# A hybrid decoder layer on one core: the up product of the MLP by Strassen's scheme, the down sums added in DRAM

## The chip, the core and the metric

The kernel runs on one core of a Trainium2 chip. The metric is the device time of one execution in microseconds; the time before is the median of three runs. A second, profiled execution gives the page and the trace that the text reads. Engines are called as the profile calls them: PE (matrix product), PEld (its weight load), DVE (vector), ACT (scalar, activations), POOL (GpSimd), SP (the queue that issues most DMAs).

## The reference

One layer over 2064 tokens (16 meta tokens and 2048 inputs) of width 1024. A first half (input projection, gated convolution, a state-space group, output projection) leaves a residual stream h. The change touches the second half only:

```
hn = rms_norm(h, norm_ffn_g)
up = causal_dwconv(hn @ w_up, ffn_conv_w, ffn_conv_b)   # 1024 -> 2 x 2816, depthwise, width 3
a, val = up[..., :2816], up[..., 2816:]                 # gate and value
h = h + (silu(a) * val) @ w_down                        # 2816 -> 1024
y = rms_norm(h, norm_final_g)[:, 16:]
```

All arrays are float32. Each product of two float32 matrices is computed as three: both factors are split into a high and a low part of type fp32r, and hi·hi, hi·lo and lo·hi are summed in PSUM.

## The kernel before

Activations lie with features on the 128 partitions and tokens along the free axis. Tokens are cut into three blocks (`BLOCKS`: 676 rows, then 688 and 688, with a halo of two carried from block to block in `halo_z`), each block into two chunks `c` of 338 or 344 columns. A matmul has a 128x128 weight tile and one chunk of columns.

Weights arrive by `Stream`: a DMA on SP into a raw tile (`wr`), a copy to fp32r on ACT (`wh`, the high part), a subtraction on DVE (`wl`, the low part). Five tiles are held ahead, two of them already split.

The MLP of a block runs over 22 tiles `f` of 128 hidden features, and for each over `i` = 0 (gate) and 1 (value). `up(f, i)` takes one weight tile, runs 8 feature groups x 2 chunks x 3 products = 48 matmuls into one PSUM tile (`product`, lines 135, 136 and 139), copies it to `z` on ACT (line 1135), and makes the convolution: one ACT operation (line 1136) and two DVE operations (`axpy`, line 111). The gate then gets Silu on ACT; the value is multiplied with it on DVE, copied to fp32r on ACT (`ah`) and subtracted on DVE (`al`).

After a chunk of hidden tiles (`FF_CHUNKS` = 6, 5, 5, 6 of the 22) the down product of that chunk runs: `down(ci, (m,))` for eight output tiles m, each 6 matmuls per hidden tile, and DVE adds each PSUM result to `acc`, a resident SBUF copy of the residual (line 105, acc<-dn,acc). The table `plan` puts this down product behind the up product of the first hidden tile of the next chunk; only the last chunk of a block has no such tile ahead of it. PSUM is held in three tiles of two banks (`ps_mm`) and two aux banks.

`prep_mlp(b + 1)` loads the next block's h, takes its norm and splits it into `h_f` and `l_f`; `finish` takes the final norm of a block from `acc` and stores y. Both are generators that `prep.step` advances a piece at a time between the products. For block 0 `prep_mlp` runs beside the last output projection of the first half, `out_block(2, ...)`. The order of the instructions on each engine is set by a scheduler from this program.

Of the kernel before, what the change touches and what calls it, by code (L numbers as in the profile page):

```python
# [50 lines left out]
FF_CHUNKS = (6, 5, 5, 6)  # L51
# [6 lines left out]
def layer_kernel(ctx, tc, xq, pk, w_in, w_glu, w_out, w_up, w_down, ssm_s, ssm_m, y):  # L58
# [8 lines left out]
    xp_ = ctx.enter_context(tc.tile_pool(name="xp_", bufs=1))  # L67
# [50 lines left out]
    def split_weights(raw, nk, name):  # L118
        hi = wp.tile([P, KD, P], F32R, tag="wh", bufs=4, name=f"wh_{name}")
        lo = wp.tile([P, KD, P], F32R, tag="wl", bufs=4, name=f"wl_{name}")  # L120
        S.activation(hi[:, :nk, :], raw[:, :nk, :], AF.Copy)  # L121
        tt(lo[:, :nk, :], raw[:, :nk, :], f32(hi[:, :nk, :]), ALU.subtract)
        return hi, lo
# [86 lines left out]

    def scaled(src, c0, rs, n, name, view=None):
# [24 lines left out]

    def norm_split(res, loads, n, cols, name):

        xs = load_halves(loads, n, name)
        yield  # L240
        yield
        rs = yield from inv_rms(xs, n, name)
        out = []
        for i, t in enumerate(xs):
            yield
            hi, lo = hl_tile(n, f"h_{name}_{i}"), hl_tile(n, f"l_{name}_{i}")
            split(t, cols[i], rs, hi, lo, n, f"{name}_{i}")
            out.append((hi, lo))
        res.append(out)
# [32 lines left out]
    prep, ssm = Side(), Side()  # L282

# [51 lines left out]
    def down_items(b, ci, tag=""):  # L335
        f0, nk = chunk_of[ci]
        return [(w_down[m, :, f0 : f0 + nk, :], nk, f"dn{b}_{ci}_{m}{tag}") for m in range(KD)]

    for b in range(3):
        for p in plan:  # L340
            if p[0] == "up":
                items.append((w_up[p[2] * FT + p[1]], KD, f"up{b}_{p[1]}_{p[2]}"))
            else:
                items += down_items(b, p[1])
        items += down_items(b, len(ends) - 1)
    items += down_items(2, len(ends) - 1, "b")
# [656 lines left out]
    def prep_mlp(b, res):  # L1003
        first, ni, _ = BLOCKS[b]
        n = ni // 2
        for c in range(2):
            s0 = first + c * n
            yield from norm_split(
                res, (h_d[:, 0:4, s0 : s0 + n], h_d[:, 4:8, s0 : s0 + n]), n, (C_FFN, C_FFN + 4), f"f{b}{c}"
            )  # L1010

    hg, hf = ([[] for _ in range(3)] for _ in range(2))
# [68 lines left out]
    prep.add(prep_mlp(0, hf[0]))  # L1081
    out_block(2, both(2), KD)
    prep.drain()
    es_2.close()


    fp = ctx.enter_context(tc.tile_pool(name="fp", bufs=1))
    ZB, MAX_OUT = 690, 688
    halo = fp.tile([P, 2 * FT, 2], F32, name="halo_z")

    def finish(b, acc, c):
        tb, ni, no = BLOCKS[b]
        n = no // 2
        halves = [acc[:, i * 4 : i * 4 + 4, c * n : (c + 1) * n] for i in range(2)]
        s = sum_squares(halves, n, f"y{b}{c}")
        yield
        rs = yield from inv_rms_of(s, D, n, f"y{b}{c}")
        yield
        s0 = tb + ni - no - META + c * n
        for k in range(KD):  # L1100
            a = acc[:, k, c * n : (c + 1) * n]
            V.scalar_tensor_tensor(out=a, in0=a, scalar=col(C_FIN + k), in1=rs, op0=ALU.mult, op1=ALU.mult)
            if k % 2 == 1:
                dma(out=y[:, k - 1 : k + 1, s0 : s0 + n], in_=acc[:, k - 1 : k + 1, c * n : (c + 1) * n])
# [12 lines left out]

    for b in range(3):
        tb, ni, no = BLOCKS[b]
        n, nn = ni // 2, no // 2  # L1120
        while len(hf[b]) < 2:
            prep.step()
        rhs = rhs_of(hf[b])
        act, br = {}, {}
        acc = None

        def up(f, i):
            t = i * FT + f
            ps = mm_tile(f"up_{b}_{f}_{i}")
# [24 lines left out]
        def down(ci, ms, cs=(0, 1)):  # L1154
# [4 lines left out]
            def rhs_down(k, i):  # L1159
                return tuple(x[:, cs[i] * nn : (cs[i] + 1) * nn] for x in act[f0 + k])  # L1160
# [8 lines left out]
        for p in plan:  # L1169
# [114 lines left out]
```

## Time and profile before

| what | us |
|---|---|
| median of 3 runs (2275.03 to 2276.7) | 2275.16 |
| the profiled execution, its own time | 2274.12 |
| its span, first to last instruction | 2272.3 |
| first `up` matmul starts at | 758.4 |
| busy in the span: PE / DVE / ACT / POOL | 2203.6 / 1329.5 / 883.2 / 34.3 |
| mean granted TensorE clock | 0.987 |

The page's groups give a line of the kernel, the engine, the operation with its tiles, the number of instructions, their busy time and the mean of one in ns, and then the idle time of the engine ahead of them with what ended it. Matmuls overlap in the records, so the mean duration of one (320 ns) is not its cost; the cost is the time of a stretch over the matmuls in it.

### The profile page before, as it was taken

The numbers are of one execution on the slowest core, as the hardware profiler recorded it, in microseconds if no ns is written. First come the engines' busy times: TensorE is split into PE (matmuls) and PEld (weight loads), VectorE is DVE, ScalarE is ACT, GpSimd is POOL, SyncE is SP. The second block draws the span as 40 slices with busy tenths as digits, with TensorE's granted clock in tenths as the row PEclk, the third lists the DMA queues.
The fourth block names the chain that finished last, engine by engine and source line by source line (L and its number), as shares of the span: only waits on it lengthen the run. The fifth ranks groups of instructions, "written<-read, shape, count | busy, mean of one in ns | idle before, by whom it ended". The sixth has DMA issues, their size and how long they took to land.

```text
span 2272.3 us, 32764 instructions
## 1 busy us (share of the span) xinstructions
PE 2203.6 (97%) x13798; PEld 2178.6 (96%) x13798; DVE 1329.5 (59%) x1911; ACT 883.2 (39%) x1175; POOL 34.3 (2%) x38
## 2 busy tenths in 40 slices
PE   4999999989899999999999999999999999999998
PEld 3998999988899999999999999999999999999997
DVE  7877499857956554444456663535356553444446
ACT  3244333227523442424244542424244442424243
POOL 0000000000000000000000000000000000000000
PEclk8999999999899999999999999999999999999999
DMA  5475444352475422231214232121223242121313
GB/s 189 121 234 146 135 146 153 116 174 65 136 241 180 167 63 77 61 88 52 88 58 132 90 133 82 54 87 54 86 61 92 90 131 84 50 90 49 91 53 118
DMA packets 134676, 245.38 MB, mean 108 GB/s; under 512 B 29120, under 2 KB 83072, under 8 KB 134400
## 3 DMA queue, kind: packets, MB, share of 16 engines
q1 hardware_dynamic: 133376, 239.05, 34.6%
q10 hardware_dynamic: 1152, 4.23, 0.5%
q8 instruction: 108, 1.77, 0.3%
q14 instruction: 40, 0.33, 0.0%
HBM read 206.94 MB, written 36.31 MB: 107 GB/s over the span
## 4 chain that ended last, share of the span: by engine, by line
PE 87%; DVE 7%; DMA 2%; ACT 2%; issue 1%; POOL 0%; SPq 0%; POOLq 0%; DVEq 0%; ACTq 0%
PE up L136 15%; PE up L135 15%; PE up L139 15%; PE dn L136 7%; PE dn L135 7%; PE dn L139 7%; PE po L135 2%; PE po L136 2%; PE po L139 2%; PE cc L136 1%; PE cc L135 1%; PE pu L136 1%; PE cc L139 1%; PE pu L139 1%; PE pu L135 1%
## 5 line engine op out<-in xcount | busy, mean ns | idle before, releaser
L135 PE MATMUL up<-h_f,wh_up 128*128 128x344 f32 (+1 forms) x2112 | 671.1, 320 | 0.0
L136 PE MATMUL up<-l_f,wh_up 128*128 128x344 f32 (+1 forms) x2112 | 669.3, 320 | 0.0
L139 PE MATMUL up<-h_f,wl_up 128*128 128x344 f32 (+1 forms) x2112 | 505.1, 318 | 0.0
L135 PEld LDWEIGHTS up<-h_f,wh_up 128*128 128x128 f32 x2112 | 397.6, 188 | 0.4
L136 PEld LDWEIGHTS up<-l_f,wh_up 128*128 128x128 f32 x2112 | 397.5, 188 | 0.4
L139 PEld LDWEIGHTS up<-h_f,wl_up 128*128 128x128 f32 x2112 | 365.7, 189 | 0.0
L135 PE MATMUL dn<-ah,wh_dn 128*128 128x344 f32 (+1 forms) x1008 | 319.8, 320 | 0.1
L136 PE MATMUL dn<-al,wh_dn 128*128 128x344 f32 (+1 forms) x1008 | 318.7, 319 | 0.0
L105 DVE TENSOR_TENSOR wl_up<-wr_up,wh_up 128x1024 fp32r<-128x1024 f32 x132 | 161.5, 1223 | 242.2 <-ACT wh_up L121 242.2
L121 ACT ACTIVATE wh_up<-wr_up 128x1024 fp32r<-128x1024 f32 x132 | 140.0, 1060 | 371.5 <-PE up L136 189.2
L111 DVE SCALAR_TENSOR_TENSOR t<-z,pv,t 128x688 f32<-128x688 f32 (+1 forms) x264 | 245.3, 929 | 66.2 <-ACT t L1136 61.9
L139 PE MATMUL dn<-ah,wl_dn 128*128 128x344 f32 (+1 forms) x1008 | 242.8, 318 | 0.0
L105 DVE TENSOR_TENSOR acc<-dn,acc 128x688 f32<-128x688 f32 (+2 forms) x104 | 84.5, 813 | 224.2 <-PE dn L139 224.2
L135 PEld LDWEIGHTS dn<-ah,wh_dn 128*128 128x128 f32 x1008 | 189.3, 188 | 0.8 <-ACT ah L1150 0.4
L136 PEld LDWEIGHTS dn<-al,wh_dn 128*128 128x128 f32 x1008 | 189.6, 188 | 0.4
L139 PEld LDWEIGHTS dn<-ah,wl_dn 128*128 128x128 f32 x1008 | 174.4, 188 | 0.0
L121 ACT ACTIVATE wh_dn<-wr_dn 128x768 fp32r<-128x768 f32 (+1 forms) x96 | 75.5, 791 | 228.4 <-PE dn L136 139.9
L105 DVE TENSOR_TENSOR wl_dn<-wr_dn,wh_dn 128x768 fp32r<-128x768 f32 (+1 forms) x96 | 85.1, 888 | 120.0 <-ACT wh_dn L121 112.0
L1136 ACT ACTIVATE t<-z,pv 128x688 f32<-128x688 f32 (+1 forms) x132 | 126.5, 959 | 1.5
L1150 ACT ACTIVATE ah<-t 128x688 fp32r<-128x688 f32 (+1 forms) x66 | 51.0, 773 | 159.1 <-DVE t L105 159.0
L1144 ACT ACTIVATE t<-t 128x688 f32<-128x688 f32 (+1 forms) x66 | 51.2, 776 | 125.7 <-DVE t L111 125.7
L121 ACT ACTIVATE wh_cw<-wr_cw 128x1024 fp32r<-128x1024 f32 x36 | 38.1, 1059 | 153.6 <-PE cc L136 44.0
(354 smaller groups left out, 3438.2 us busy)
## 6 DMA issues: line engine op xcount, KB each, us to landing
wr_up<-in_w_up SPq DMA_DIRECT2D x132, 512.0 KB, 3.5
wr_cw<-in_w_in SPq DMA_DIRECT2D x36, 512.0 KB, 4.6
wr_dn<-in_w_down SPq DMA_DIRECT2D x48, 384.0 KB, 3.2
wr_dn<-in_w_down SPq DMA_DIRECT2D x48, 320.0 KB, 2.9
x_c<-in_xq SPq DMA_DIRECT2D x16, 688.0 KB, 4.7
xr<-in_xq SPq DMA_DIRECT2D x24, 344.0 KB, 4.0
h_d<-xr SPq DMA_DIRECT2D x24, 344.0 KB, 3.2
wr_o<-in_w_out SPq DMA_DIRECT2D x16, 512.0 KB, 4.9
```

Of the source, the lines that this page charges most:

```text
L105: V.tensor_tensor(out, a, b, op=op)
L111: V.scalar_tensor_tensor(out=out, in0=a, scalar=s, in1=b, op0=ALU.mult, op1=ALU.add)
L121: S.activation(hi[:, :nk, :], raw[:, :nk, :], AF.Copy)
L135: T.matmul(ps[c], hi[:, k, :], xh, start=k == 0, stop=False)
L136: T.matmul(ps[c], hi[:, k, :], xl, start=False, stop=False)
L139: T.matmul(ps[c], lo[:, k, :], xh, start=False, stop=k == nk - 1)
L1136: S.activation(a, z[:, nz - no :], AF.Identity, scale=col(C_FW + 2 * 44 + t), bias=col(C_FB + t))
L1144: S.activation(a, a, AF.Silu)
L1150: S.activation(hi, a, AF.Copy)
```

## The change

The up product of one hidden tile is now a 2x2 block product: rows are gate and value, the inner dimension is the lower and the upper four of the eight feature groups, columns are the two token chunks. Strassen's scheme in Winograd's form makes it with seven half products instead of eight. Each half product (`form`) is 4 feature groups x 3 products = 12 matmuls of one chunk, so a hidden tile has 84 matmuls instead of 96. For this

- the seven right factors b11, t1, t2, b21, t3, t4, b22 are made once per block from the four quarters of the normed block (`prep_mlp`), and each is split into two fp32r parts held in 14 tiles `xf`;
- the seven left factors are made for each hidden tile: four DMAs bring the weights into three raw tiles, four DVE additions of 128x512 make the sums (`Pair.sums`), and three tiles of 1024 columns and one of 512 (`w4`) are split, where two of 1024 were;
- the results are put together outside PE: three ACT copies and four DVE additions from PSUM for each hidden tile (`up`), instead of two ACT copies. One partial sum in PSUM (X) is read by ACT while its accumulation goes on later; Y is read likewise by DVE.

The sign of the value row is taken into negated convolution weights (`pneg`). `Feed` replaces `Stream` in the MLP: at most three raw and four split tiles, refilled as a split tile is released. PSUM is two tiles of two banks (`xy`), two of one bank (`pz`) and the two aux banks. The work behind the up product of a hidden tile (`activate`) is a generator in three parts that runs within the next hidden tile's forms.

The hidden tiles are cut into chunks of 4, 4, 4, 3, 3 and 4, and a chunk's down product follows its own last up product (`settle` first); its first two output tiles share the loop (`first_pair`), so that the chunk's last hidden tile comes last in both. The result of a down product is no longer added by DVE to an SBUF tile: ACT copies it to `ev` (two buffers), and a DMA issued by POOL adds it to h in DRAM (`accum_op`). Only the last chunk of the last block still adds in SBUF. `finish` and the norm of the next block (`prep_rs`) read h back from DRAM. `prep_mlp` of block 0 cannot run beside `out_block(2, ...)` any more: its tiles lie in pools opened after that.

```diff
-FF_CHUNKS = (6, 5, 5, 6)
+FF_CHUNKS = (4, 4, 4, 3, 3, 4)
...
+    prep.add(prep_rs(0))
     out_block(2, both(2), KD)
     prep.drain()
     es_2.close()
+    es_x.close()
+    es_ps.close()
...
+    xf = ctx.enter_context(tc.tile_pool(name="xf", bufs=1, side="right"))
     fp = ctx.enter_context(tc.tile_pool(name="fp", bufs=1))
+    ps_xy = ctx.enter_context(tc.tile_pool(name="ps_xy", bufs=2, space=bass.MemoryType.PSUM))
+    ps_z = ctx.enter_context(tc.tile_pool(name="ps_z", bufs=2, space=bass.MemoryType.PSUM))
...
+        def sums(self):
+            self.t.append(fp.tile([P, 4, P], F32, tag="w4", bufs=1, name=f"w4_{self.name}"))
+            t = self.t
+            tt(t[0][:, 4:8, :], t[2][:, 4:8, :], t[2][:, 0:4, :], ALU.add)
+            tt(t[1][:, 0:4, :], t[0][:, 4:8, :], t[0][:, 0:4, :], ALU.add)
+            tt(t[2][:, 4:8, :], t[2][:, 4:8, :], t[0][:, 0:4, :], ALU.add)
+            tt(t[3], t[1][:, 0:4, :], t[1][:, 4:8, :], ALU.add)
...
+        def done(k, a):
+            hi, lo = (xf.tile([P, 4, QM], F32R, tag="xf", bufs=14, name=f"{w}_{k}_{b}")[:, :, :n] for w in "hl")
+            parts(a, hi, lo)
+            res[k] = (hi, lo)
...
+        done("b11", a)
+        tt(a, a, b12, ALU.subtract)
+        done("t1", a)
...
+        def form(ps, w, h, k, start=True, stop=True):
+            hi, lo = (a[:, h * 4 : h * 4 + 4, :] for a in w)
+            xh, xl = x[k]
+            for j in range(4):
+                kw = dict(skip_group_check=not (start and stop))
+                T.matmul(ps, hi[:, j, :], xh[:, j, :], start=start and j == 0, stop=False, **kw)
+                T.matmul(ps, hi[:, j, :], xl[:, j, :], start=False, stop=False, **kw)
+                T.matmul(ps, lo[:, j, :], xh[:, j, :], start=False, stop=j == 3, **kw)
...
+        def up(f):
...
+            w0 = feed.take()
+            form(X, w0, 0, "b11", stop=False)
+            S.activation(g2[:, 0, :], X, AF.Copy)
+            work()
+            form(Y, w0, 1, "t1", stop=False)
+            feed.done()
+            w1 = feed.take()
+            form(X, w1, 0, "t2", start=False, stop=False)
+            S.activation(g2[:, 1, :], X, AF.Copy)
+            work()
+            form(z1, w1, 1, "b21")
+            tt(g2[:, 0, :], z1, g2[:, 0, :], ALU.add)
+            feed.done()
+            w2 = feed.take()
+            form(X, w2, 1, "t3", start=False)
+            S.activation(v2, X.unsqueeze(1).to_broadcast([P, 2, n]), AF.Copy)
+            tt(v2[:, 1, :], Y, v2[:, 1, :], ALU.add)
+            work()
+            form(z2, w2, 0, "t4")
+            tt(v2[:, 0, :], z2, v2[:, 0, :], ALU.add)
+            feed.done()
+            w3 = feed.take()
+            form(Y, w3, 0, "b22", start=False)
+            tt(g2[:, 1, :], Y, g2[:, 1, :], ALU.add)
+            feed.done()
+            later.append(activate(f, (g, v)))
...
-                a = two(acc[:, m, :])[:, cs[0] : cs[-1] + 1, :]
-                tt(a, ps[:, cs[0] : cs[-1] + 1, :nn], a, ALU.add)
...
+                if into is None:
+                    ev = ev2_tile(f"ev_{b}_{ci}_{m}")[:, :no]
+                    S.activation(two(ev), ps[:, :, :nn], AF.Copy)
+                    G.dma_start(out=h_d[:, m, s0 : s0 + no], in_=ev, accum_op=ALU.add)
...
+            for f in range(f0, f0 + nk):
+                up(f)
+            settle()
+            if ci < last:
+                for ms in first_pair:
+                    down(ci, ms)
+                    prep.step(2 * len(ms))
```

Two places show how the order moves. The first is PE at the end of a chunk in block 1. Before, chunk 1 is hidden tiles 6 to 10; these rows are the end of the value product of tile 11 and the start of the down product dn, whose right factors are `ah` and `al` of tiles 6 and on:

```order
L139 MATMUL up_11_1_12985<-h_f_1_10904,wl_up_11_1_12855 128x344
L135 MATMUL dn_1_0_0_13053<-ah_6_12037,wh_dn_1_0_12922 128x344
...
L135 MATMUL dn_1_0_0_13053<-ah_10_12917,wh_dn_1_0_12922 128x344
L136 MATMUL dn_1_0_0_13053<-al_10_12918,wh_dn_1_0_12922 128x344
L135 MATMUL dn_1_0_0_13053<-ah_10_12917,wh_dn_1_0_12922 128x344
```

Between the last product of tile 10 and the down product stand the 96 matmuls of tile 11. With the change, chunk 2 is tiles 8 to 11 and the same place reads as follows:

```order
L1331 MATMUL xy_11_13768<-h_b_1_11446,wl_up_11_3_13763 128x344
L136 MATMUL dn_2_0_0_13922<-ah_8_13584,wh_dn_2_0_13803 128x344
...
L140 MATMUL dn_2_0_0_13922<-ah_10_13862,wl_dn_2_0_13804 128x344 x2
L136 MATMUL dn_2_1_0_13923<-ah_8_13584,wh_dn_2_1_13841 128x344
...
L140 MATMUL dn_2_1_0_13923<-ah_10_13862,wl_dn_2_1_13842 128x344 x2
L136 MATMUL dn_2_0_0_13922<-ah_11_13918,wh_dn_2_0_13803 128x344
L136 MATMUL dn_2_1_0_13923<-ah_11_13918,wh_dn_2_1_13841 128x344
L137 MATMUL dn_2_0_0_13922<-al_11_13919,wh_dn_2_0_13803 128x344
```

The down product now needs tile 11 itself, and 36 matmuls (tiles 8 to 10 for two output tiles) stand between its last up matmul and the first use of `ah` of tile 11; in a chunk of three it is 24.

The second place is DVE within a hidden tile. Before, in block 1, this is what stands there for tile 9 (two weight tiles split, four `axpy`, the product and the low part):

```order
L105 TENSOR_TENSOR wl_up_11_0_12791<-wr_up_11_0_12594,wh_up_11_0_12790 128x1024
L111 SCALAR_TENSOR_TENSOR t_9_0_12713<-z_9_0_12712,pv,t_9_0_12713 128x688 x2
L105 TENSOR_TENSOR wl_up_11_1_12855<-wr_up_11_1_12662,wh_up_11_1_12854 128x1024
L111 SCALAR_TENSOR_TENSOR t_9_1_12777<-z_9_1_12776,pv,t_9_1_12777 128x688 x2
L105 TENSOR_TENSOR t_9_1_12777<-t_9_0_12713,t_9_1_12777 128x688
L105 TENSOR_TENSOR al_9_12786<-t_9_1_12777,ah_9_12785 128x688
```

With the change, the stretch from the sums of tile 11's weights to the last addition from PSUM of tile 10:

```order
L107 TENSOR_TENSOR w_up_11_13662<-wr_up_11_1_13567 128x512
L107 TENSOR_TENSOR wl_up_11_0_13668<-wr_up_11_0_13529,wh_up_11_0_13667 128x1024
L107 TENSOR_TENSOR z_10_0_13625<-pz_10_0_13628,z_10_0_13625 128x344
L107 TENSOR_TENSOR wl_up_11_1_13706<-wr_up_11_1_13567,wh_up_11_1_13705 128x1024
L107 TENSOR_TENSOR v_9_13643<-g_9_13644,v_9_13643 128x688
L107 TENSOR_TENSOR z_10_1_13626<-xy_10_13627,z_10_1_13626 128x344
L1231 SCALAR_TENSOR_TENSOR v_b_2_15624<-v_b_2_15624,pv,rsk_1_13267 128x344
L107 TENSOR_TENSOR al_9_13727<-v_9_13643,ah_9_13726 128x688
L107 TENSOR_TENSOR z_10_1_13626<-pz_10_1_13629,z_10_1_13626 128x344
L107 TENSOR_TENSOR wl_up_11_2_13744<-wr_up_11_2_13605,wh_up_11_2_13743 128x1024
L107 TENSOR_TENSOR z_10_0_13625<-xy_10_13627,z_10_0_13625 128x344
L107 TENSOR_TENSOR wl_up_11_3_13763<-w_up_11_13662,wh_up_11_3_13762 128x512
```

One queue now carries the weights of the next tile, the additions that PE waits for (z from xy, whose bank PE goes on with), the multiplication and split of the tile before, and here a scaling for block 2 (v_b).

More of the change, by code (lines that the diff above doesn't have):

```diff
@@ L235, in load_halves @@
         return xs
[L237 to L249, printed above, removed]
     def norm_group(res, src, n, c0, name, **kw):
@@ L1001, in prep_ssm @@
         res.append(((hi, lo),))
[L1003 to L1012, printed above, removed]
+    hg = [[] for _ in range(3)]
     xh2 = dict(pool=a2, tag="xhl2", bufs=8)
@@ L1080, in layer_kernel, with prep_rs @@
     prep.lanes = 1
-    prep.add(prep_mlp(0, hf[0]))
+    rs_f = [{} for _ in range(3)]
+    def prep_rs(b):
+        first, ni, _ = BLOCKS[b]
+        n = ni // 2
+        for c in range(2):
+            out = cp.tile([P, QM], F32, tag="rsk", bufs=2, name=f"rsk_{b}_{c}")[:, :n]
+            s0 = first + c * n
+            rs_f[b][c] = yield from inv_rms_from([h_d[:, i * 4 : i * 4 + 4, s0 : s0 + n] for i in range(2)], n, f"f{b}{c}", out)
+            yield
+    prep.add(prep_rs(0))
     out_block(2, both(2), KD)
@@ L1092, in finish, with y_at @@
+    def y_at(b, c):
         tb, ni, no = BLOCKS[b]
         n = no // 2
[L1094 to L1104, printed above, removed]
@@ L1118, in layer_kernel, with z_tile, ev2_tile @@
+    def z_tile(name):
+        return fp.tile([P, ZB], F32, tag="z", bufs=4, name=name)
+    def ev2_tile(name):
+        return fp.tile([P, MAX_OUT], F32, tag="ev2", bufs=2, name=name)
+    prep.add(prep_rs(1))
+    hf = [{} for _ in range(3)]
+    feed.pump()
+    finish_gens(prep_mlp(0, hf[0]))
+    acc = []
     for b in range(3):
@@ new lines, in work @@
+        def work():
+            if later and next(later[0], prep) is prep:
+                later.popleft()
+        def up(f):
+            g, v = (z_tile(f"z_{b}_{f}_{i}")[:, :nz] for i in range(2))
+            g2, v2 = two(g[:, o:]), two(v[:, o:])
+            xy = xy_tile(f"xy_{b}_{f}")
+            X, Y = xy[:, 0, :n], xy[:, 1, :n]
+            z1, z2 = (ps_z.tile([P, 512], F32, tag="z", name=f"pz_{b}_{f}_{i}")[:, :n] for i in range(2))
+            w0 = feed.take()
[24 more added lines that the diff above has]
+            later.append(activate(f, (g, v)))
+            if b == 2 or "scaled" not in hf[b + 1]:
+                prep.step(2 if f0_last <= f else 1)
@@ L1186, in layer_kernel @@
             for ms in first_pair:
                 down(last, ms)
[L1188 to L1204 removed]
+                prep.step(len(ms))
```

346 lines of the change are left out of this document (248 added, 98 removed).

## The prediction

> **What bounds the kernel now.** I read the page first: its list of busy times, its groups, its chain. Then I asked the trace for the busy time by stretches of the MLP.
>
> ```profile
> PE up L136 15%; PE up L135 15%; PE up L139 15%; PE dn L136 7%; PE dn L135 7%; PE dn L139 7%; PE po L135 2%; PE po L136 2%; PE po L139 2%; PE cc L136 1%; PE cc L135 1%; PE pu L136 1%; PE cc L139 1%; PE pu L139 1%; PE pu L135 1%
> ...
> L135 PE MATMUL up<-h_f,wh_up 128*128 128x344 f32 (+1 forms) x2112 | 671.1, 320 | 0.0
> ```
> ```profile
> core 0: us, PE busy (x) PEld busy (x) DVE busy (x) ACT busy (x) POOL busy (x), PEclk, DMA share, GB/s
> ...
> 760.00:1260.00 500.00, 500.00 (x3240) 499.55 (x3239) 253.40 (x281) 198.97 (x274) 1.70 (x2) 1.00 0.27 83
> 1260.00:1760.00 500.00, 500.00 (x3172) 499.22 (x3171) 260.21 (x303) 195.60 (x309) 3.40 (x4) 1.00 0.27 83
> 1760.00:2260.00 500.00, 499.28 (x3161) 498.19 (x3159) 252.64 (x301) 192.04 (x277) 3.14 (x3) 1.00 0.28 83
> 2260.00:2272.00 12.00, 2.68 (x12) 1.58 (x12) 4.19 (x9) 0.94 (x2) 0.85 (x1) 0.61 0.33 117
> ```
>
> The chain that ended last is PE, and two thirds of it are the up and down products. From 760 to 2260 us PE has no gap but 0.7 us, at full clock; DVE and ACT are busy half and two fifths of it. So matmuls taken out come off the end, for as long as PE stays fed. A matmul costs the stretch over its count: 500 / 3240 = 0.1543 us in the first stretch (mostly 338 columns), 500 / 3172 = 0.1576 us in the second (344 columns).
>
> **What is removed.** Each hidden tile loses 12 matmuls, and there are 22 tiles in each of three blocks: 264 at 0.1543 and 528 at 0.1576 are 40.7 + 83.2 = **124 us**. The up product has three groups of 2112 in the page; 792 of these 6336 go. The down product keeps its number. DVE also loses its additions to `acc`, which costs or gains nothing while DVE is off the path.
>
> **DVE within a hidden tile.** PE now takes 84 x 0.1576 = 13.2 us for a tile. What DVE does in that time is priced from these groups (mean in ns) and from the starts in a busy stretch:
>
> ```profile
> L111 DVE SCALAR_TENSOR_TENSOR t<-z,pv,t 128x688 f32<-128x688 f32 x176 | 164.5, 934 | 44.3 <-ACT t L1136 41.5
> ...
> L105 DVE TENSOR_TENSOR wl_up<-wr_up,wh_up 128x1024 fp32r<-128x1024 f32 x118 | 144.3, 1223 | 217.4 <-ACT wh_up L121 217.4
> ...
> L105 DVE TENSOR_TENSOR l_f<-t_f,h_f 128x1376 fp32r<-128x1376 f32 x8 | 12.7, 1589 | 0.0
> ...
> L105 DVE TENSOR_TENSOR acc<-dn,acc 128x344 f32<-128x344 f32 x16 | 8.1, 513 | 6.6 <-PE dn L139 6.6
> ```
> ```profile
> 1270.83 0.85 DVE L105 TENSOR_TENSOR sq_y<-sq_y 128x672 f32<-128x672 f32 x1
> 1271.60 0.93 DVE L111 SCALAR_TENSOR_TENSOR t<-z,pv,t 128x688 f32<-128x688 f32 x1
> 1272.44 0.50 DVE L105 TENSOR_TENSOR sq_y<-sq_y 128x336 f32<-128x336 f32 x1
> 1272.86 0.87 DVE L105 TENSOR_TENSOR t<-t,t 128x688 f32<-128x688 f32 x1
> 1274.09 1.23 DVE L105 TENSOR_TENSOR wl_up<-wr_up,wh_up 128x1024 fp32r<-128x1024 f32 x1 [0.35 <-ACT wh_up L121]
> 1275.23 0.87 DVE L105 TENSOR_TENSOR al<-t,ah 128x688 fp32r<-128x688 f32 x1
> ```
>
> From start to start (1270.83 to 1271.60 and so on) an operation that waits for nothing costs some 0.08 us less than its mean: 0.77 for 672 columns, 0.84 for an axpy of 688, 0.42 for 336, 1.14 for 1024. An estimate between these gives 0.61 for 512. A tile now has four sums (2.44), three splits of 1024 and one of 512 (4.03), four additions of 344 from PSUM (1.72), four axpys (3.38), the product and the low part (1.56): **13.1 us, against 13.2 on PE**. By the means, which is what operations cost that each wait for another engine, it is 14.6. Which of the two holds decides this change. I take 13.1 plus the waits, since the queue has much that is free to go; both ends stay in the range.
>
> It is not so in every tile of a chunk. The first has its weights made during the down product ahead of it, where DVE has room; the last has no next tile's sums. That leaves 2 + 2 + 2 + 1 + 1 + 2 = 10 full tiles a block. I laid such a tile's rows in their order beside PE: the addition from Y, on which PE's last form waits, ends 0.3 us ahead of that form, and the addition after the form comes round again after 13.4 us, 0.2 later than on PE. That is 10 x 0.2 = 2 us a block, and what else falls there adds in full. A block has some 48 us of such other DVE work (16 scalings, 12 operations like the l_f row, two sums of squares, the final scaling); I put 15 us of it into full tiles and half of that on the path. So 3 x (2 + 7) = **27 us** is lost; 8 if all is hidden, 69 if a full tile takes the means (30 x 1.4 + 27).
>
> ACT has 3.5 splits, three copies, two convolutions, Silu and `ah`, by its groups under 10 us of 13.2; it is not the bound.
>
> **The end of a chunk.** Before, the 96 matmuls of another tile lie between a chunk's last up product and its down product. Now 36 do (5.7 us), or 24 (3.8 us). What they must hide is priced by the one place before where nothing lies between, the end of the last block; in the chain in order of time:
>
> ```profile
> 2213.57 0.97 ACT t L1136
> 2214.57 0.95 DVE t L111
> 2215.54 0.95 DVE t L111
> 2216.51 0.89 DVE t L105
> 2217.41 0.79 ACT ah L1150
> ```
> ```profile
> L1144 ACT ACTIVATE t<-t 128x688 f32<-128x688 f32 x44 | 34.3, 780 | 86.0 <-DVE t L111 86.0
> ```
>
> These are 4.55 us. Silu is new in this chain (0.78; before, it was the gate that came first), and so is the addition from PSUM ahead of it (0.51): 5.8 us at the least. In DVE's queue that addition stands behind one axpy (0.5 late), and a split and an axpy of the value delay the gate's by some 0.4 more, so `ah` is there after 6.7 us and `al` after 7.6. PE waits 1.5 us with 36 matmuls ahead of it (1.0 for `ah`, 0.5 for `al`), 3.4 with 24: 4 x 1.5 + 2 x 3.4 = 12.8 us a block. In the last chunk of blocks 0 and 1 the next block's factors add some 2 us, and in the last of block 2, with half the matmuls ahead, 3: 3 x 12.8 + 7 = **45 us**. The least is 20 (5.8 us), the most 80 (9 us, with DVE behind).
>
> **Eviction and the adding DMA.** PSUM for the down product has two buffers where it had three. The third output tile waits for the first's copy, which stands behind a split on ACT: 0.3 us in each of 18 chunks, **5 us** (0 to 10). The copy after next waits until the DMA has read its buffer, so a DMA may take two output tiles less a copy (0.73): 2 x 24 x 0.1576 - 0.73 = 6.8 us in a chunk of four, 5.0 in a chunk of three. Nothing of this kind is in the trace before; the nearest rows are plain DMAs of this size:
>
> ```profile
> xr<-in_xq SPq DMA_DIRECT2D x24, 344.0 KB, 4.0
> h_d<-xr SPq DMA_DIRECT2D x24, 344.0 KB, 3.2
> ...
> x_f<-h_d SPq DMA_DIRECT2D x8, 688.0 KB, 4.7
> ```
>
> A write is 3.2 us; a read and then a write 7.2. I take a value near the write, under 5, so **0 us**; at 7.2 the chunks of three lose some 5 us each, 28 in all. The Trainium skill, page "DMA: Bandwidth & Descriptors", section "Anatomy of one DMA — SWDGE (gpsimd) path", gives a DMA issued by GpSimd 2.0 us and its bytes over 436 GB/s, by estimate 2.8 us here, and does not price the adding; the sum would be the same.
>
> **The start of the MLP.** Before, the first factors were made beside the last output projection, and PE ran through. Now everything from the last po matmul stands in a row: the addition (0.88), its write to h (3.2 above, since the new pools wait for it), the load of a quarter (4.7), four scalings, the high part.
>
> ```profile
> 739.24 3.94 DVE L216 SCALAR_TENSOR_TENSOR t_f<-x_f,pv,rs_f 128x338 f32<-128x338 f32 x8 [1.48 <-ACT rs_f L208]
> ```
> ```profile
> L223 ACT ACTIVATE h_f<-t_f 128x1376 fp32r<-128x1376 f32 x8 | 10.9, 1359 | 12.9 <-DVE t_f L216 12.9
> ```
>
> 0.9 + 3.2 + 4.7 + 2.0 + 1.4 = 12.2 us until the first matmul. Then DVE sets the pace: 12 more scalings (5.9), five sums and seven low parts (12 x 1.55 = 18.6), and about 3 us of the next tile's weights, some 28 us until the last form, which takes 1.9: about 42 us, in which PE can do its 84 matmuls and some 20 of the next tile, 16 us. Lost: **26 us** (20 to 35).
>
> **The end.** The tail is built as before; I add 2 us for single rows where pairs were scaled, and 3 for the clock after gaps (below). None of these terms can go below nothing, since PE has no other idle time to win. The sum: -124 + 27 + 45 + 5 + 0 + 26 + 2 + 3 = **-16 us**. It is made against the profiled execution, 2274.1; the median is 2275.2, so the forecast is 2274.1 - 16 = 2258 in round numbers.
>
> **The rivals.**
>
> *PE stays fed.* DVE does have room as a mean over the MLP (13.1 of 13.2 only in full tiles), and PE and DVE can drift by a few us. With 8 for DVE, 20 for the start, 30 at the chunks and 4 of the rest: -124 + 62, **2212**. Against it: PE's forms wait for single additions, so drift helps little.
>
> *DVE becomes the bound, and the kernel is slower.* The place is the DVE queue of a full tile, where each addition from PSUM waits for PE or ACT and holds what stands behind it. If waiting operations cost their means, 14.6 us, and the other work comes on top, it is 69 for the 27: -124 + 69 + 45 + 5 + 26 + 5 = +26, **2300**. It decides the sign from about 43 us on, that is 13.9 us a full tile. For it: 14.6 is what the groups say; against it: starts in the busy stretch lie closer.
>
> *The adding DMA holds the eviction.* At 7.2 us the sum is -16 + 28, **2286**; at 10 us, by the same count, over 2350. For it: the operation reads its target too. Against it: DMA is busy only 27% in these stretches.
>
> *The clock.* Gaps of PE let its clock fall, as at the start of the kernel:
>
> ```profile
> 34.00:38.00 4.00, 0.74 (x7) 0.69 (x7) 2.69 (x16) 0.00 (x0) 0.87 (x1) 0.91 0.00 0
> 38.00:42.00 4.00, 1.51 (x2) 0.49 (x2) 3.25 (x18) 0.46 (x1) 0.00 (x0) 0.50 0.00 0
> ...
> 46.00:50.00 4.00, 4.00 (x15) 4.00 (x15) 4.00 (x30) 2.27 (x2) 0.00 (x0) 0.50 0.47 150
> ```
>
> After some 4 us almost idle the clock is 0.50, and still so through 4 busy us. If each of 18 chunk ends cost 4 us at half clock, it is 36 more, **2291**. I expect it at the start of the MLP alone, where DVE hides most of it: 3 us. The skill's page "TensorE: Matmul & The Clock Gate", section "What's actually happening", puts the fall at one idle window of about 3.4 us; by that rule waits of 1.5 us keep the clock and those of 3.4 are on the edge, which is between my sum and this rival, and the rows above agree with it.
>
> That the change doesn't remove the work is ruled out by the order: 84 matmuls stand in each tile.
>
> **How the numbers follow.** Forecast (2235 to 2278) 0.42; PE stays fed 0.22; DVE bound 0.18; adding DMA 0.10; clock 0.08. A measurement of this kernel can tell about 0.2%, 4.5 us. Of the forecast 0.30 is faster, 0.08 same, 0.04 slower; PE fed is all faster; of DVE bound 0.15 is slower, 0.02 same, 0.01 faster; the DMA is all slower; of the clock 0.06 slower, 0.01 each of the others. Faster 0.54, same 0.11, slower 0.35. The range leaves out the lower half of PE fed, and the far ends of DVE bound and of the DMA: 2212 to 2318.
>
> **What would show it.** In the profile after: 792 fewer PE matmuls; waits of PE on ACT `ah` and DVE `al` at L136 and L137 of 1 to 4 us, 18 times; DVE at 90% or more in the up stretches and PE's first Y matmul after it waiting; one gap of about 12 us ahead of the first xy; POOL's DMAs landing in under 5 us. If PE's waits in the up stretches name DVE in every tile, the DVE rival holds; if ACT's `ev` waits for DMA, the other. A down product that starts without a wait would make my largest loss wrong.

## The result, and the profile after

The kernel became slower: 2347.95 us, median of four runs (2343.85 to 2353.18), against 2275.1 for the kernel before beside it; the ratio is 1.0322 with a 95% interval of [1.0299, 1.0344]. The profiled execution took 2349.42, 75.3 more than that of before. The forecast was 2258.

The page of after: the busy times, the chain, the groups and the DMA issues that matter here.

```profile
PE 2157.9 (92%) x13012; PEld 2096.0 (89%) x13012; DVE 1664.8 (71%) x2561; ACT 1117.8 (48%) x1579; POOL 152.1 (6%) x174
...
issue 42%; PE 34%; DVE 9%; DMA 8%; POOL 4%; ACT 3%; SPq 0%; POOLq 0%; DVEq 0%; ACTq 0%
...
L1414 ACT ACTIVATE ev<-dn 128x688 f32<-128x688 f32 (+1 forms) x136 | 99.9, 734 | 133.3 <-DMA h_d<-ev 112.4
...
wr_up<-in_w_up SPq DMA_DIRECT2D x264, 256.0 KB, 3.7
h_d<-ev POOLq DMA_DIRECT2D x88, 344.0 KB, 6.1
```

The work did go: the up product has 5544 matmul records instead of 6336, 792 fewer (786 fewer in all, since the norms have six more). PE is busy 92% of the span; before, it was 97%. The chain that ended last was this before:

```profile
PE 87%; DVE 7%; DMA 2%; ACT 2%; issue 1%; POOL 0%; SPq 0%; POOLq 0%; DVEq 0%; ACTq 0%
```

Now PE is 34% of it and 42% is "issue", time in which the engine waited for nothing that the profile shows, so the chain doesn't say where the time went. The stretches of the MLP do (columns as in the prediction): the start, two full tiles inside a chunk, the end of a chunk of three, the end of a chunk of four, and what follows the last up product.

```profile
758.40:809.95 51.55, 31.31 (x157) 29.43 (x156) 40.84 (x52) 24.31 (x27) 0.00 (x0) 0.70 0.49 160
1419.60:1446.10 26.50, 26.50 (x170) 26.50 (x169) 25.67 (x36) 17.66 (x33) 0.00 (x0) 1.00 0.31 90
...
1612.20:1658.10 45.90, 39.02 (x230) 37.16 (x228) 21.80 (x30) 19.95 (x32) 6.92 (x8) 0.96 0.61 127
1538.40:1585.40 47.00, 45.02 (x277) 43.50 (x277) 23.25 (x32) 20.38 (x33) 6.92 (x8) 1.00 0.60 131
2291.20:2347.70 56.50, 40.12 (x220) 37.18 (x219) 36.12 (x72) 27.53 (x48) 1.73 (x2) 0.83 0.32 102
```

- **Two full tiles** take 26.5 us: 168 matmuls at 0.1576. Nothing is lost, although DVE is busy 25.67 of 26.5.
- **The start**: 84 + 72 matmuls at 0.1543 are 24.1 us, and it took 51.55: 27.4 lost.
- **The end of a chunk**, taken from the end of form t4 of the chunk's last tile to that of the next tile: 84 + 144 matmuls are 35.9 us, and 45.9 passed, 10.0 lost; with four tiles 84 + 192 are 43.5 of 47.0, 3.5 lost. Taken so from the timeline, the 17 ends that have a next tile last 833.7 us and hold 688.9 us of matmuls: **145 us lost**, 3.5 to 13.6 each (62 small matmuls of the norms count as lost here). The forecast had some 50 for all 18.
- **The last stretch**: 192 matmuls, 30.3 us of 56.5, 26 lost. Before, 288 matmuls, 45.4 us, stood in the 60.0 us behind the last up product, 15 lost.

Nearly all that the forecast lacks is lost at the ends of chunks (145 us against some 50).

What PE, ACT and DVE waited for from 756 us on (waits: total us, times, longest):

```profile
PE dn L136 <- ACT ah L242: 40.4, 17, 4.1
PE dn L136 <- ACT ev L1414: 21.3, 28, 2.4
PE xy L1329 <- ACT z L1367: 11.9, 10, 2.2
PE xy L1329 <- ACT h_b L242: 11.1, 1, 11.1
PE xy L1329 <- DVE z L107: 7.6, 4, 3.2
PE xy L1329 <- ACT z L1373: 5.1, 6, 1.4
...
PE dn L137 <- DVE al L107: 3.4, 11, 0.3
```
```profile
DVE wr_up L107 <- DMA wr_up<-in_w_up: 193.0, 40, 11.2
```

The waits for `ah` and `al` (43.8) are those that were forecast (45). New are some 24 us on `ev` and 25 us in the first two tiles behind a down product, on copies of X and additions that come late. At the end of the chunk of three above, DVE and ACT do this (start, us, what, idle before it and what ended it):

```profile
1631.92 0.56 DVE L107 TENSOR_TENSOR wl_dn<-wr_dn,wh_dn 128x384 fp32r<-128x384 f32 x1 [3.20 <-ACT wh_dn L242]
1638.85 1.42 DVE L107 TENSOR_TENSOR wr_up<-wr_up 128x512 f32<-128x512 f32 x2 [6.37 <-DMA wr_up<-in_w_up]
```
```profile
1637.89 0.74 ACT L1414 ACTIVATE ev<-dn 128x688 f32<-128x688 f32 x1 [4.31 <-DMA h_d<-ev]
1639.58 2.01 ACT L242 ACTIVATE wh_up<-wr_up 128x1024 fp32r<-128x1024 f32 x2 [0.94 <-DVE wr_up L107]
...
1647.73 0.74 ACT L1414 ACTIVATE ev<-dn 128x688 f32<-128x688 f32 x1 [2.01 <-DMA h_d<-ev]
1648.37 0.45 ACT L1367 ACTIVATE z<-xy 128x344 f32<-128x344 f32 x1
```

Two things stand in one queue on ACT: evictions that wait for adding DMAs, and splits of the next tile's weights that wait for DVE's sums, which wait for loads. The loads can start only as the down product's raw tiles come free (the last `wl_dn` at 1631.92, the last two of the four loads at 1632.51 and 1632.89), since `Feed` has three raw tiles for both; they then run beside the adding DMAs. The first copy of X of the next tile stands behind all that.

### The profile page after: what moved, and what is told of

The parts are those of the page before. It is cut to its first block, busy times and chain, and to the rows that moved or that the text cites. A ratio compares the mean times of both kernels' runs of the same rounds, so it can differ in the third digit from the quotient of the medians.

```text
span 2347.7 us, 33350 instructions
## 1 busy us (share of the span) xinstructions
PE 2157.9 (92%) x13012; PEld 2096.0 (89%) x13012; DVE 1664.8 (71%) x2561; ACT 1117.8 (48%) x1579; POOL 152.1 (6%) x174
## 3 DMA queue, kind: packets, MB, share of 16 engines
q0 software_dynamic: 19584, 47.52, 13.1%
## 4 chain that ended last, share of the span: by engine, by line
issue 42%; PE 34%; DVE 9%; DMA 8%; POOL 4%; ACT 3%; SPq 0%; POOLq 0%; DVEq 0%; ACTq 0%
POOL h_d L1415 4%; PE xy L1329 2%; PE xy L1330 2%; PE xy L1331 2%; PE po L136 2%; PE po L137 2%; PE po L140 2%; DMA wr_up<-in_w_up 2%; DMA h_d<-ev 2%; PE dn L137 1%; PE dn L136 1%; PE dn L140 1%; PE pu L137 1%; PE cc L140 1%; PE cc L137 1%
## 5 line engine op out<-in xcount | busy, mean ns | idle before, releaser
L136 PE MATMUL dn<-ah,wh_dn 128*128 128x344 f32 (+1 forms) x1024 | 337.0, 335 | 61.8 <-ACT ah L242 40.4
L1329 PE MATMUL xy<-h_t,wh_up 128*128 128x344 f32 (+1 forms) x792 | 260.8, 329 | 20.3 <-ACT z L1367 11.9
L1330 PE MATMUL xy<-l_t,wh_up 128*128 128x344 f32 (+1 forms) x792 | 255.1, 322 | 1.5 <-DVE l_t L107 1.5
L1331 PE MATMUL xy<-h_t,wl_up 128*128 128x344 f32 (+1 forms) x792 | 254.5, 321 | 0.0
L1329 PE MATMUL xy<-h_b,wh_up 128*128 128x344 f32 (+1 forms) x528 | 171.2, 329 | 23.7 <-ACT h_b L242 11.1
L1415 POOL DMA_DIRECT2D h_d<-ev x136 | 118.2, 869 | 1063.1 <-ACT ev L1414 1060.8
L1329 PEld LDWEIGHTS xy<-h_t,wh_up 128*128 128x128 f32 x792 | 150.7, 190 | 33.3 <-ACT z L1367 20.5
L1330 PE MATMUL xy<-l_b,wh_up 128*128 128x344 f32 (+1 forms) x528 | 172.3, 326 | 3.8 <-DVE l_b L107 3.8
L1331 PE MATMUL xy<-h_b,wl_up 128*128 128x344 f32 (+1 forms) x528 | 171.9, 326 | 0.3 <-DVE wl_up L107 0.3
L1330 PEld LDWEIGHTS xy<-l_t,wh_up 128*128 128x128 f32 x792 | 150.8, 190 | 1.9 <-DVE l_t L107 1.9
L1331 PEld LDWEIGHTS xy<-h_t,wl_up 128*128 128x128 f32 x792 | 151.0, 191 | 0.0
```

Of the source, the lines that this page charges most:

```text
L136: T.matmul(ps[c], hi[:, k, :], xh, start=k == 0, stop=False)
L1329: T.matmul(ps, hi[:, j, :], xh[:, j, :], start=start and j == 0, stop=False, **kw)
L1330: T.matmul(ps, hi[:, j, :], xl[:, j, :], start=False, stop=False, **kw)
L1331: T.matmul(ps, lo[:, j, :], xh[:, j, :], start=False, stop=j == 3, **kw)
L1415: G.dma_start(out=h_d[:, m, s0 : s0 + no], in_=ev, accum_op=ALU.add)
```

## The experiments

Three causes were held apart: **A**, the adding DMA holds its two `ev` buffers; **B**, the wait for `ah` at a chunk's end; **C**, the loads of the weights are late. All ratios are to the kernel before (2274 to 2275 beside each). Kernels e2, e7, y1 and z1 leave the addition to h out. Those with own raw tiles also hold one `rs` tile (the norm's scale) instead of two.

| run | what | us | ratio, 95% interval |
|---|---|---|---|
| (the change) | | 2347.95 | 1.0322 [1.0299, 1.0344] |
| e1_ev3 | three `ev` | 2347.28 | 1.0328 [1.0303, 1.0354] |
| e2_plain | plain DMA, other array | 2304.81 | 1.0133 [1.0118, 1.0148] |
| z1_plain_h | plain DMA into h | 2301.23 | 1.0114 [1.0101, 1.0128] |
| e3_later | down one tile later | 2303.42 | 1.0127 [1.0112, 1.0142] |
| e4_later_ev3 | e3 + three `ev` | 2301.85 | 1.0124 [1.0108, 1.0139] |
| e5_ev3_first | e1 + eviction ahead of split | 2364.22 | 1.0403 [1.0384, 1.0422] |
| e6_later_ev3_first | e5 + e3 | 2301.27 | 1.0115 [1.0098, 1.0131] |
| e7_later_first_plain | e6 + plain | 2237.75 | 0.9840 [0.9826, 0.9855] |
| x4_wrd | own raw tiles for down | 2330.30 | 1.0236 [1.0219, 1.0253] |
| y1_wrd_plain | x4 + plain | 2292.06 | 1.0083 [1.0066, 1.0100] |
| y2_wrd_ev3 | x4 + three `ev` | 2324.21 | 1.0218 [1.0203, 1.0234] |
| z3_wrd_ev3_pool | y2 + POOL reads | 2331.88 | 1.0250 [1.0234, 1.0266] |
| x2_fill | idle PE filled | 2337.52 | 1.0269 [1.0250, 1.0287] |
| e8_later_first_wrd | e3 + first + own raw tiles | 2279.42 | 1.0017 [1.0007, 1.0026] |
| y3_later_wrd_ev3 | e8 + three `ev`, 8 tiles for `ah` and `al` | 2276.77 | 1.0012 [1.0002, 1.0022] |
| x3_five | e8, five chunks | 2256.44 | 0.9916 [0.9901, 0.9931] |
| z2_five_pool | x3 + POOL reads | 2271.92 | 0.9992 [0.9983, 1.0001] |
| x1_before_adds | before + adding DMAs | 2274.06 | 0.9994 [0.9984, 1.0003] |

**A third eviction buffer.**

```diff
-        return fp.tile([P, MAX_OUT], F32, tag="ev2", bufs=2, name=name)
+        return fp.tile([P, MAX_OUT], F32, tag="ev2", bufs=3, name=name)
```

> One change: three eviction buffers (ev) instead of two. The profile of after has PE waiting 21.3 + 2.6 us for ACT ev and another 24.6 us for ACT z and DVE z at the first tile behind a down product, and ACT ev waiting 112.4 us for the adding DMA, which lands after 6.1 us. Theory A (the adding DMA with two buffers holds ACT, so PSUM, so PE, and the first copies of X behind it): three buffers leave a DMA 10.6 us (chunks of four) and 7.8 us (chunks of three), so nearly all of that 48 us goes, and some 10 of the clock lost behind it: 2348 - 58 = 2290. Theory B (the wait for ah at the end of a chunk, and the clock that falls in it, are the loss; ACT's wait for the DMA lies beside it): 2335 to 2348. Theory C (weights arrive late: DVE's sums wait 193 us for the loads of w_up): 2340 to 2350.

Nothing gained (2347.28). ACT's wait for the DMA is gone in e1, but PE's wait on `ev` stayed, at 25.0 us:

```profile
ACT ev L1414 <- DMA h_d<-ev: 0.6, 2, 0.4
```

ACT's timeline of e1 at the same chunk end shows why:

```profile
1632.47 0.75 ACT L1414 ACTIVATE ev<-dn 128x688 f32<-128x688 f32 x1 [1.79 <-PE dn L140]
1637.10 2.00 ACT L242 ACTIVATE wh_up<-wr_up 128x1024 fp32r<-128x1024 f32 x2 [3.89 <-DVE wr_up L107]
1639.02 0.72 ACT L1414 ACTIVATE ev<-dn 128x688 f32<-128x688 f32 x1
```

The eviction at 1639.02 now waits behind the weights. A alone is out.

**The addition left out**, once into another array and once into h.

```diff
-                    G.dma_start(out=h_d[:, m, s0 : s0 + no], in_=ev, accum_op=ALU.add)
+                    G.dma_start(out=sc_d[:, m, s0 : s0 + no], in_=ev)
```

> One change: the DMA that POOL issues writes ev plainly to another DRAM array of h's shape; the down sums are not added to h, so the output lacks them. Bytes written, buffers and order stay. Theory A1 (the adding makes the DMA slow: a read and a write): landing falls from 6.1 to 3 to 4 us, ACT ev hardly waits for DMA, and the time falls as with three buffers, to some 2290. Theory A2 (a DMA issued by POOL is slow in itself, or the DMA engines are loaded by the weights): landing stays at 5 us or more and the time within 15 us of 2348. Theories B and C: time within 15 us of 2348 whatever the landing.

> The change with plain DMAs into h itself (e2 wrote to another array), so that the sums replace h instead of being added: all waits on h stay as in the change, only the adding goes. Theory G (a good part of the 43 us was the wait of finish's reads for the sums, which e2 removed): 2315 to 2330. Theory H (it is the adding: longer DMAs that fill the DMA engines): as e2, 2300 to 2310.

2304.81 and 2301.23: the adding costs **43 to 47 us**, and the waits on h's order, which z1 keeps, are no part of it. All waits of PE on `ev` and `z` together fall from 48.6 us to 15.9 in e2, and DVE's for the loads from 193 to 132. The DMA view of the 40 us in which the down product of that chunk runs, first of after, then of e2 (queue: packets, MB, share of 16 engines; issues: KB each, us to landing):

```profile
q0 software_dynamic: 1152, 2.82, 45.2%
q1 hardware_dynamic: 1674, 3.00, 24.2%
...
wr_up<-in_w_up SPq DMA_DIRECT2D x12, 256.0 KB, 4.7
h_d<-ev POOLq DMA_DIRECT2D x8, 344.0 KB, 6.0
```
```profile
q0 software_dynamic: 640, 2.82, 17.4%
...
wr_up<-in_w_up SPq DMA_DIRECT2D x12, 256.0 KB, 3.7
sc_d<-ev POOLq DMA_DIRECT2D x8, 344.0 KB, 3.8
```

The same eight transfers of 2.82 MB take 45.2% of all 16 engines' time where they add and 17.4% where they write: 40 x 0.452 / 8 = 2.3 us of all engines for each, against 0.9. The loads beside them land after 4.7 us instead of 3.7.

**The down product one hidden tile later**, without and with the other edits.

```diff
             for f in range(f0, f0 + nk):
                 up(f)
-            settle()
-            if ci < last:
-                for ms in first_pair:
-                    down(ci, ms)
+                if f == f0 and ci:
+                    for ms in first_pair:
+                        down(ci - 1, ms)
...
+            if ci == last:
+                settle()
```

> One change: the down product of a chunk comes one hidden tile later, behind the first tile of the next chunk (the weights' order is changed to suit), except for the last chunk of a block. 15 of 18 waits for ah should go. Theory B: 36 of the 44 us of waits for ah and al, and with them most of the clock lost at chunk ends (some 38 us by the half-clock windows): 2348 - 70 = 2278. Theory A: the waits for ah go but the waits for ev and the slow start behind the down product stay, with their clock: 2348 - 36 - 10 = 2302. Theory C: the waits only move to the sums: 2335 to 2350.

> Both: three eviction buffers, and the down product one hidden tile later. If A and B are both right and add up, with the clock lost at chunk ends gone too: 2348 - 48 - 36 - 35 = 2229, faster than before (2275). If one of them hides the other: no better than the better of the two alone, 2278 to 2300. Theory C: 2335 to 2350.

2303.42, near the 2302 of theory A: B is worth **45 us** for 15 of the 18 ends, with the clock and what comes late behind it. PE's wait for `ah` falls from 40.4 us to 10.0 and the clock between the start and the tail rises from 0.97 to 0.99, but the wait on `ev` in the down product grows from 21.3 us to 37.0. The third buffer again adds nothing (2301.85). e5 and e6 put the eviction ahead of the split in the program:

```diff
             for m, ps, _ in todo:
-                feed.done()
...
                     S.activation(two(ev), ps[:, :, :nn], AF.Copy)
...
+                feed.done()
```

> Three eviction buffers, and in the program the eviction stands ahead of the next weights' split (which the release of a weight tile sets off) instead of behind it. In e1 ACT ev no longer waits for its DMA, but ACT wh_up waits 125.5 us for DVE wr_up (the sums), with ev behind it, and DVE waits 191.6 us for the loads of w_up: PE's 25.0 us on ev stayed. Theory D1 (the order on ACT's queue is what makes the late loads cost time): the 25 + 3 us and some clock go: 2315. Theory D2 (the loads of w_up are themselves the limit behind a down product, and what does not wait for ev then waits for the weights or for the copies of X behind them): 2335 to 2348.

> As e5, and the down product one hidden tile later. Compared with e4 (2302): D1 takes its 36.5 us of waits for ev and gives 2265; D2 gives 2290 to 2302.

> As e6, with plain DMAs into another DRAM array for the adding ones (the down sums are not added to h). If the loads are late because the adding DMAs take the DMA engines' time (45.2% of 16 engines in 40 us at a chunk end of after, against 17% by the same bytes written plainly in e2), this is what is left without it: D2 gives some 2250 (2302 less most of the 43 us that e2 gained); if the order on ACT is the whole cost (D1), within 10 us of e6.

e5 is slower than the change (2364.22) and e6 no better than e4: what no longer waits for `ev` waits for the copies of X (26.1 us on `z` at L1373 in e5). The order on ACT isn't the cause. e7 shows both causes together: 64 us below e6, and 110 below the change, more than 45 + 43.

**Raw tiles of their own for the down product**, so that the three raw tiles load the next hidden tile before the adding starts.

```diff
-            self.raw, self.loaded = load_weights(*self.args), True
+            src, nk, name = self.args
+            raw = fp.tile([P, 4, P], F32, tag="wrd", bufs=2, name=f"wr_{name}")
...
+            self.loads = [deque(j for j in jobs if isinstance(j, c)) for c in (Down, PairTile)]
+            self.limit, self.raw = (2, 3), [0, 0]
```

> The change with one thing altered: the raw weights of the down product in two tiles of their own, so that the next hidden tile's raw weights are loaded ahead of the down product. Order of the down product, order of the eviction and its two buffers as in the change. D2 (late loads behind the adding DMAs): DVE's wait for w_up falls from 193 us to about 64 as in e8, and the time by some 20 to 40: 2308 to 2328. If the two eviction buffers or the wait for ah hold it all the same: 2335 to 2350.

> The change with raw tiles of their own for the down product (x4, 2330) and plain DMAs into another DRAM array (e2, 2305; the down sums are not added to h). Theory E (the late loads are late through the adding): the own raw tiles have little left to gain, 2295 to 2305. Theory F (the shallow feed costs 18 us by itself, beside the adding): 2305 - 18 = 2287.

> x4 with three eviction buffers (and 8 instead of 10 tiles for ah and al, to make room; in the change a chunk of four fills 8). The adding DMAs stay. Theory E: with the loads out of the way, ACT's wait for the adding DMA (82.9 us in x4) is what is left, and three buffers now gain most of the 25 us between x4 and e2: 2305 to 2312. Theory F: as in e1, nothing: 2325 to 2335.

> y2 (2324) with the reads of h for the final norm issued by POOL instead of SP. Theory G: 20 us less, 2300 to 2308. Theory H: at most 5 less, 2318 to 2326.

2330.30: C is worth **18 us**; 13 of them remain without any adding (y1 against e2), so neither expectation for y1 was right: the shallow feed costs by itself. Whether a little of it goes through the adding (18 less 13) is within the intervals. DVE's wait for the loads falls from 193 us to

```profile
DVE wr_up L107 <- DMA wr_up<-in_w_up: 62.9, 22, 6.0
```

With the loads early, a third buffer gains 6 at the most (y2, the intervals overlap; its `ah` and `al` have 8 tiles instead of 10 to make room). The adding still costs 38 (x4 against y1) or 32 (y2 against y1). Nothing is won by taking the final norm's reads of h out of SP's queue: issued by POOL (z3) they make it 8 slower.

**The adding DMAs in the kernel before.** Its order and its five weight tiles ahead stay; h is not read there again.

```diff
                 tt(a, ps[:, cs[0] : cs[-1] + 1, :nn], a, ALU.add)
+                if ci < len(ends) - 1:
+                    s0 = tb + ni - no
+                    for _ in range(2):
+                        G.dma_start(out=h_d[:, m, s0 : s0 + no], in_=acc[:, m, :], accum_op=ALU.add)
```

> The kernel before, with DMAs that POOL issues added behind each down product but those of the last chunk of a block: each row of acc is added twice to h in DRAM, where it is not read again (144 adding DMAs, 136 in the change). Order, acc and the five weight tiles held ahead stay. If the adding DMAs cost by filling the DMA engines while the change holds only one hidden tile's raw weights (D2), the deep feed of before bears them: 2274 to 2290. If they cost wherever they run (PE or the other engines slowed, or the weights late with any feed), the price of e2 and e7 comes back: 2274 + 43 to 64 = 2317 to 2338.

2274.06, ratio 0.9994 [0.9984, 1.0003]: 144 adding DMAs cost nothing. They land after 6.1 us as in the change, the DMA engines are busy 0.49 instead of 0.27 in the MLP, and PE has no gap:

```profile
760.00:1260.00 500.00, 500.00 (x3239) 499.55 (x3239) 253.22 (x282) 198.23 (x273) 43.94 (x50) 1.00 0.49 116
1260.00:1760.00 500.00, 500.00 (x3172) 499.22 (x3171) 259.60 (x303) 195.46 (x307) 45.49 (x52) 1.00 0.49 116
```

So here the adding slows neither PE nor DVE. In this kernel five weight tiles lie ahead, DVE has room, and PSUM doesn't wait for a DMA; which of these makes it free was not tried apart.

**The clock.** Matmuls that nobody reads fill PE's wait for `ah`.

```diff
+                if len(ms) > 1 and ks[0] == 0:
+                    fill = aux_tile(f"fill_{b}_{ci}")[:, :nn]
+                    w0 = act[f0][0]
+                    for _ in range(25 if ci == last else 20 if nk == 3 else 10):
+                        T.matmul(fill, w0[:, :P], w0[:, :nn], start=True, stop=True)
```

> The change, with matmuls that nobody reads put on PE where it waits for ah at a chunk end: 20 of 344 columns in chunks of three, 10 in chunks of four, 25 in the last chunk of a block (3.2, 1.6 and 3.9 us, about as long as the waits in the profile). They add 270 matmuls in time that was idle. If the clock's fall behind such a wait costs what the half-clock windows say (77 us of half clock at the chunk ends, so up to 38 us, of which I give these waits 20 to 30), the time falls to some 2320 to 2330 although work is added. If the fall costs nothing on the path, 2345 to 2360.

2337.52: with 285 matmuls more (by the trace; the expectation counts 270) the kernel is 10 us **faster**. The waits for `ah` are off PE's list, and the clock over the stretch between the start and the tail, first of after, then of x2 (last three columns: clock, DMA share, GB/s), rises by 0.02 (rounded), which over 1467 us is some 29 us of matmuls at full speed:

```profile
809.95:2289.30 1479.35, 1384.05 (x8418) 1348.81 (x8419) 1037.80 (x1434) 773.87 (x1189) 126.17 (x144) 0.97 0.49 119
```
```profile
805.20:2272.40 1467.20, 1400.04 (x8679) 1364.76 (x8679) 1037.27 (x1433) 769.51 (x1189) 125.80 (x144) 0.99 0.49 120
```

Less than this came out at the end, and less than the 20 to 30 expected; PE's waits on `ev` rose from 21.3 to 29.0 us and those on DVE's `z` from 7.6 to 11.9, as if an earlier PE met the DMAs earlier.

**Towards a faster kernel.** e8 is the later down product, eviction first and the own raw tiles (two `ev`). x3 is e8 with `FF_CHUNKS = (4, 5, 4, 5, 4)`, that is 112 adding DMAs. y3 is e8 with a third buffer, z2 is x3 with the final norm's reads issued by POOL.

> The down product one tile later, eviction first, two eviction buffers as in the change; the raw weights of the down product get two tiles of their own, so that the three raw tiles hold the next hidden tile's weights through the whole down product (loaded ahead of the adding DMAs). The adding DMAs stay. D2: DVE's wait for w_up (190 us) falls under 60 and the time to 2250 to 2275. D1: little more than e6.

> e8 (2279) with three eviction buffers and 8 tiles for ah and al. Theory E: 2279 - 25 = 2254. Theory F: 2272 to 2282.

> As e8, with five chunks of 4, 5, 4, 5 and 4 hidden tiles instead of six: 112 adding DMAs instead of 136, three interruptions of the up products fewer, and more time per output tile for a DMA. By e7 against e6 the adding costs 64 us at 136, of which e8 took back 22: 42 x 24 / 136 = 7, and the fewer ends some 3 to 6: 2266 to 2270 from 2279, under before (2274). If the chunks' number does not matter: 2275 to 2282.

> x3 (2256) with the reads of h for the final norm issued by POOL instead of SP. Theory G: 2240 to 2246. Theory H: 2251 to 2258. Before is 2274 to 2275.

e8 is at 2279.42, y3 at 2276.77 (3 us by the buffer, within the intervals, not 25). x3 reaches **2256.44, 0.9916 [0.9901, 0.9931]**: faster than both kernels, by more than expected (23 us under e8, not 9 to 13). Its PE waits 2.2 us for `ev` in the down product where e8 waited 11.2 (all waits on `ev`: 8.8 against 13.9), so the longer chunks also give the DMAs time:

```profile
PE dn L136 <- ACT ev L1419: 2.2, 8, 0.6
```

z2 is worse again (2271.92), and why is not shown. A read of h stands on POOL for 54.7 us at the longest:

```profile
POOL sq_y L217 <- DVE wr_up L107: 60.7, 2, 54.7
```

But that read leaves at 1339.73 and the next eviction starts at 1348.34, so it holds no adding DMA; the two that leave latest behind their eviction do so after 2.2 and 2.5 us. PE's wait on `ev` in the down product is 13.0 us again.

## Why the prediction was wrong

**What is removed: right.** 792 matmuls went, and a full tile takes 13.25 us, the 84 x 0.1576 that was forecast.

**DVE within a hidden tile (27): the size right by luck, the place wrong.** All but a few tiles lose 0.0 to 0.3 us each, also with DVE 97% busy, so the lower of the two prices (13.1) held, and the rival in which DVE becomes the bound fell. The tiles that are no chunk's end lost 27.6 us in all by the same count from the timeline, but 19.4 of it in four: the third tile of the MLP (6.4), and second tiles of chunks early in blocks 1 and 2 (6.1, 3.8, 3.1), where the reads and the norm of `finish` for the block before run beside them.

**The end of a chunk (45): right as a wait**, 43.8 us in the profile, and e3 takes 45 off the time for 15 of 18 ends. In the chunk of four shown above PE waits 1.3 us for `ah` and 0.3 for `al`, in the chunk of three 3.0 and 0.3; 1.5 and 3.4 were forecast for the two together. The 45 of e3 has the clock in it, which I had booked elsewhere and too low.

**Eviction and the adding DMA (5 + 0): the step that failed.** Its words were "a value near the write, under 5, so 0 us". The DMA lands after 6.1 us, so the value was wrong, and the place was wrong too. I asked only whether a transfer is done before its buffer is needed; by that count 6.1 us costs a little in chunks of three, and a third buffer would have brought it back. e1 shows that it doesn't. PE waits 24 us on `ev` where 5 were forecast, and 25 more on `z`. In its place the runs show the adding itself: the same bytes written plainly take 43 to 47 us off (e2, z1), and 64 with the down product one tile later (e7 against e6). An adding DMA takes 2.3 us of all 16 engines instead of 0.9, in a stretch where the loads of the next weights run on the same engines and land later (4.7 us against 3.7). That the engines' time is the link fits all of this, but it was not varied by itself. The rival "the adding DMA holds the eviction" had the right culprit, and its mechanism, the buffer alone, fell with e1. Its ground against itself, that DMA is busy only 27%, was a mean of before; at the ends it is 0.6 of all engines now.

**The term that was missing: the feed.** I counted DVE's work on the next tile's weights and never asked when their loads may start. Three raw tiles shared with the down product let them start only near its end: 18 us (x4), 13 of them without any adding (y1). Before held five tiles ahead, and there the same adding DMAs cost nothing (x1), though DVE also had more room there and no eviction waited for them.

**The start (26): right**, 27.4, with a gap of 11.1 us where 12.2 was forecast.

**The end (2, and 3 in the last chunk): too low.** The last stretch loses 26 us where it lost 15 before.

**The clock (3): too low.** The clock of 0.97 over the 1479 us between the start and the tail is by estimate some 40 us of matmuls at full speed, the size of the clock rival (36), though part of that time PE waits anyway; x2 shows 10 us, net, for the waits for `ah`. The waits of 3 us that I called on the edge did lower it: the trace shows 0.96 in the chunk of three with its wait of 3.0 us and 1.00 in the chunk of four with 1.3. The Trainium skill's rule (page "TensorE: Matmul & The Clock Gate", section "What's actually happening": one idle window of about 3.4 us) comes near these two, though 3.0 is less than 3.4 already. It doesn't fit the whole trace: behind a wait of 1.9 us that ended at 1722.92, PE had been busy 1.49 of the 3.4 us up to 1723.9, and the clock was 0.51 in the 3.4 us after.

**What stays open.** With early loads the adding still costs 38 us (x4 against y1), 32 with a third buffer (y2 against y1). The traces say where PE meets it: its waits on `ev` and `z` together are 32.0 us in x4, 26.6 in y2 and 7.2 in y1, and from 756 us on its clock is at half for 111 us in x4, 112 in y2 and 87 in y1. Part of it goes through the loads still. In y2 DVE waits 78.5 us for the loads of w_up against 43.2 in y1, and behind six of its seven waits of 4.9 us and more (the longest in y1 is 4.5) PE waits for a copy of X that stands behind the weights on ACT, 7.7 us in all:

```profile
1132.87 1.42 DVE L107 TENSOR_TENSOR wr_up<-wr_up 128x512 f32<-128x512 f32 x2 [6.03 <-DMA wr_up<-in_w_up]
```
```profile
1133.64 1.06 ACT L242 ACTIVATE wh_up<-wr_up 128x1024 fp32r<-128x1024 f32 x1 [5.52 <-DVE wr_up L107]
1134.60 0.43 ACT L1375 ACTIVATE z<-xy 128x338 f32<-128x338 f32 x1
```
```profile
1135.09 0.42 PE L1331 MATMUL xy<-h_t,wh_up 128*128 128x338 f32 x1 [1.71 <-ACT z L1375]
```

The largest single difference is the end of block 1's first chunk (13.2 us lost against 5.7), where `finish` reads h as well. How much each of these is worth by itself was not tried by a run.

## What to carry to other kernels

A DMA that takes the place of a DVE addition is not free just because the DMA engines look idle on average: price it in engine time, in the stretch where it runs, and list what else must arrive there. When a change makes room by holding fewer tiles ahead, follow each load from the moment its buffer comes free. And where a theory names a buffer, try one more buffer first: one run showed here that the buffer alone was not the cause.

## What the runs showed of the hardware

An adding DMA of 336 or 344 KB from SBUF to DRAM landed after 5.4 to 6.3 us (medians of a run), a plain one issued by POOL in the same place after 3.8 to 4.1 (3.4 with early loads), and an adding one took 2.6 times the engines' time (45.2% against 17.4%) in 144 packets instead of 80. The Trainium skill (page "DMA: Bandwidth & Descriptors", section "Anatomy of one DMA — SWDGE (gpsimd) path") gives the plain one by estimate 2.8 us; the measurement is higher, beside the loads that run with it. And work added to an idle PE made a kernel 10 us faster (x2), with the clock at 0.99 instead of 0.97 between the start and the tail.
